# A two-layer hybrid encoder: 24 of the modulation sums of layer 0 move from VectorE to TensorE, beside the attention heads

## The chip, the cores and the metric

One Trainium2 chip, one of its cores. The metric is the device time of one execution in microseconds (us), the median of several executions. A core has TensorE (PE in the rows; its weight loads PEld), VectorE (DVE), ScalarE (ACT), GpSimd (POOL) and SyncE (SP); here SP only issues transfers. Each engine takes its instructions in the order in which the program was built.

## The reference

512 tokens of width 1024, two layers. Each layer takes six vectors from the conditioning `c`, 1024 wide each, that is 48 chunks of 128 numbers:

```python
c_act = jax.nn.silu(c)
mod = c_act @ w_mod[l] + b_mod[l]                 # 1024 -> 6144
sh1, sc1, g1, sh2, sc2, g2 = split(mod, 6)        # chunks 0-7, 8-15, 16-23, 24-31, 32-39, 40-47
h = rmsnorm(x, norm1[l]) * (1 + sc1) + sh1
u = h @ w_in[l]                                   # A: latent attention, B: dilated attention, C: S5
x = x + g1 * (concat(norm(o_a), norm(o_b), norm(o_c)) @ w_out[l])
h2 = rmsnorm(x, norm2[l]) * (1 + sc2) + sh2
x = x + g2 * conv_ffn(h2, ffn_w_up[l], ..., ffn_w_down[l])
```

So the first 16 chunks of layer 0 are wanted before the input projection, chunks 16 to 39 only after the attention: g1 when the output projection is added to x, sh2 and sc2 in the norm behind it.

## The kernel before

Activations lie transposed, 128 channels on the partitions and 512 tokens along a row. Every large product is three TensorE products of split operands (`mm3`, lines 378 to 380: high by high, low by high, high by low). A weight block comes by DMA into a `raw` tile (3 buffers), ScalarE casts its high part `wh` (line 372) and VectorE or GpSimd subtracts the low part `wl` (line 373); `wh` and `wl` have 4 buffers each.

A layer runs: input projection in three groups of output tiles (`u` in the rows; the first group has 6 output tiles and `w_in` blocks of 768 columns, the second 5 tiles and blocks of 640, the third 3 and 384), the S5 branch beside it (`bp`, `cp`, `bt`, `tm` are its tables, which go out to memory and come back; `oc` goes out and comes back as `U`; `s5s`, `s5y` are its products), six attention steps `n` of two heads each (dilated for n = 0 to 2, latent for n = 3 to 5), the output projection (`wo`), the norm and the feed-forward part. An attention step does, per 128 queries and head, scores (`sc`), the softmax pieces on VectorE and ScalarE (`P`, `nb`), four transposes (`pt`) and, per half, the product with the values (`pv`); `finish_pair` ends the step with a product on VectorE (line 1159, `ob` or `oa`). The work of the next heads is written beside each half (`side`).

The modulation sums are made in two ways:

- `mod_chunk` (line 328): a chunk of 128 columns comes in by a 512 KB transfer and one VectorE instruction multiplies it by the spread `c_act` and sums it. Chunks 16 to 39 of layer 0 are handed to `mixing` as `background`, two at a time: 12 are written in steps n = 3 to 5 (through `raw`), 12 beside the output projection (through `rawm`).
- `quad_rows` and `quad_cols` (lines 341 and 352): four chunks at once. Eight TensorE products `mq` take one column of `c_act`, 32 columns wide, against a 128x512 block of weights and add up in one bank; ScalarE copies the row out (`mrow`), four small products `mc` turn it into columns, two VectorE additions put in the bias. This is done for chunks 0 to 15, the 4 entries of `QUADS`: entry 0 ahead of the first group of the input projection, the others inside it by a rule on the block number `k`:

```python
q = k // 2 + 1
if q < len(QUADS) and k % 2 == 0 and i1 == nt:
    row, cur["pe"] = quad_rows(q, e)
elif q < len(QUADS) and k % 2 and i0 == 0:
    cur["pe"] = quad_cols(q, row, e)
```

The order on every engine is set when the program is built, by a scheduler that goes by priorities (`PRI`, `low(...)`) and by its own reckoning of when an instruction can start. On the chip each queue then runs in that order, and a transfer that waits for a buffer holds back all that are behind it on SP.

Of the kernel before, what the change touches and what calls it, by code (L numbers as in the profile page):

```python
# [11 lines left out]
F32R = mybir.dt.float32r  # L12
# [9 lines left out]
KD = D // 128  # L22
NH = 6
NPAIR = 22
PRI = {"xs": -400, "U1": 300, "ws": -200, "rs": -300, "cu": 10, "fin": 20, "glu": -30, "par": -30,
       "prep1": -20, "qk": 20, "rope": -20, "spread": -30}
MK = 2
OWN = 6
TOGETHER = 300
DQ = (0, 3, 0, 0)  # L30
QUADS = tuple((8 + 2 * q, 9 + 2 * q, 2 * q, 2 * q + 1) for q in range(4))
BLOCKS = ((0, 8), (8, 15), (15, 22))
EPS = 1e-6
MAGIC = 12582912.0
# [187 lines left out]
def program(ctx, tc, a, out):  # L222
    nc = tc.nc
# [34 lines left out]
    def as32(x):  # L258
        return x.bitcast(F32)
# [71 lines left out]
    def quad_rows(q, e):  # L331


        o = ps("mq")
        p_, nb = cur["modraw"]
        for t in range(4):
            r = p_.tile([128, 1024], F32, tag="rawm", name="rawm", bufs=nb)
            nc.sync.dma_start(r, a["wquad"][q, t])
            for k in (2 * t, 2 * t + 1):
                with after(e):  # L340
                    m = T.matmul(o[k % 4 * 32:k % 4 * 32 + 32], cth[:, k:k + 1].to_broadcast([128, 32]),
                                 r[:, k % 2 * 512:k % 2 * 512 + 512], start=k < 4, stop=k >= 4).ins
        row = p_.tile([128, 512], F32, tag="mrow", name="mrow", bufs=2)
        S.copy(row, o)
        return row, m

    def quad_cols(q, row, e):

# [449 lines left out]
    def mixing(l, background):  # L798
# [465 lines left out]
        def side(n):  # L1264

            if n == 0:
                for _ in range(2):
                    with low("dq"):
                        ahead.append(dil_qk(len(ahead)))
                    yield  # L1270
            elif n == 1:
                with low("qk"):
                    ahead.append(next_qk(0))
                with low("glu"):
                    s5_glu(l, mp, oc)
                yield
                with low("qk"):
                    ahead.append(next_qk(1))
            elif n == 2:
                with low("mc"):  # L1280
                    mix_group("mc", [oc[:, 0], oc[:, 1]], 6, (6, 7, 8, 9))
                yield
                with low("va"):
                    va.append(mla_values())
                with low("qk"):
                    ahead.append(next_qk(2))
            elif n == 3:
                with low("qk"):
                    ahead.append(next_qk(3))
                yield  # L1290
                with low("mb"):
                    mix_group("mb", ob, 3, range(6))
            elif n == 4:
                with low("qk"):
                    ahead.append(next_qk(4))
                yield
                with low("qk"):
                    ahead.append(next_qk(5))
            while True:
                yield  # L1300

        va = []
        for n in range(6):
            pr = n % 3
            sums = ap.tile([128, 8], F32, tag="sums", name="sums", bufs=2)
            o = ps("pv", "pv")
            beside = side(n)
            for half in range(2):
                PT = pt_tiles()
                for qt in (2 * half, 2 * half + 1):  # L1310
                    if n < 3:
                        S2 = scores2(*ahead[n], qt)
                    for hh in range(2):
                        if n < 3:
                            args = S2[hh], -0.125, K("bias", 384 - 128 * qt, 512)
                        else:
                            q, k, qs = ahead[3 + 2 * pr + hh]
                            args = scores(q, k, qt), qs[:, qt:qt + 1], None
                        unit(*args[:2], qt, hh, PT[hh], sums[:, hh * 4 + qt:hh * 4 + qt + 1], args[2])
                if n >= 3:  # L1320
                    background(2)
                with low("pv"):
                    pv(o[:, half * 256:half * 256 + 256], PT, dv if n < 3 else va[0], pr, half == 0, half == 1)
                catch_up()
                next(beside)
                catch_up()
            catch_up()
            if n >= 3:
                oa[pr] = ap.tile([128, N], F32, tag=f"ob{pr}", name=f"oa{pr}")
            with low("fin"):  # L1330
                finish_pair(o, sums, (oa if n >= 3 else ob)[pr])
# [217 lines left out]
    for l in range(L):  # L1549
        mod = lambda i, j0, j1: [lambda j=j: mod_chunk(i, j) for j in range(j0, j1)]  # L1550
        first = l == 0
        later = bg(mod(0, 16, 40) if first else [])
        mixing(l, later)
        later(100)
        nxt = bg((mod(0, 40, 48) if first else []) + (mod(l + 1, 0, 48) if l + 1 < L else []))
        ffn(l, nxt, prep(l + 1) if l + 1 < L else iter(()))
# [21 lines left out]
```

## Time and profile before

| | us |
|---|---|
| median of three timed runs | 1512.4 (1510.29 to 1515.06) |
| the profiled execution, its own time | 1503.78 |
| its span in the trace | 1502.0 |
| TensorE busy | 1394.0 (93%) |
| VectorE busy | 1040.3 (69%) |
| ScalarE busy | 693.0 (46%) |
| granted TensorE clock, mean | 0.961 of full speed |

The last 1.8 us of the profiled execution lie outside the span. Times of the trace are us from the span's start. A busy TensorE need not be at its peak, since the ends of pipelined products are modelled; the pitch from one start to the next tells how long one holds the engine.

### The profile page before, as it was taken

How to read it: one execution, taken by the hardware profiler on the slowest of the kernel's cores; microseconds unless marked ns; L12 is line 12 of the kernel's file. 1: busy time of each engine (PE TensorE's matmuls, PEld its weight loads, DVE VectorE, ACT ScalarE, POOL GpSimd, SP SyncE). 2: the span in 40 equal slices, each digit the busy share in tenths (PEclk: the TensorE clock that was granted, in tenths of full speed). 3: DMA queues.
4: the chain of work that ended last, by engine and by line, in shares of the span. 5: the costliest groups of instructions: out<-in, count | busy, mean ns of one | idle time of the engine just before them, and what ended most of it. 6: DMA issues, size and time to landing. Idle time of an engine off the chain costs nothing. (4 is left out here: it accounts for less than half of the span.)

```text
span 1502.0 us, 20427 instructions
## 1 busy us (share of the span) xinstructions
PE 1394.0 (93%) x7260; PEld 1120.1 (75%) x7260; DVE 1040.3 (69%) x2122; ACT 693.0 (46%) x1351; POOL 342.3 (23%) x290
## 2 busy tenths in 40 slices
PE   6889889888899999999999988898899999999998
PEld 3677656658878778887888766566698888888887
DVE  6687888856698779788647585667548663663663
ACT  4464365652454434444446335666445432442441
POOL 1274241310222153242134343223110000000000
PEclk9889999989999999999999999999999999999999
DMA  7746323105556477386336332000041333323322
GB/s 259 238 150 207 96 61 118 58 1 173 170 184 213 137 243 250 113 252 207 103 110 196 92 118 80 19 18 10 9 131 57 98 98 89 96 93 102 99 90 93
DMA packets 79398, 185.11 MB, mean 123 GB/s; under 512 B 12864, under 2 KB 38208, under 8 KB 79296
## 3 DMA queue, kind: packets, MB, share of 16 engines
q1 hardware_dynamic: 77856, 181.37, 38.2%
q10 hardware_dynamic: 1440, 2.44, 0.5%
q8 instruction: 57, 0.93, 0.3%
q14 instruction: 45, 0.37, 0.1%
HBM read 165.95 MB, written 15.73 MB: 121 GB/s over the span
## 5 line engine op out<-in xcount | busy, mean ns | idle before, releaser
L372 ACT CAST wh<-raw 128x512 fp32r<-128x512 f32 (+3 forms) x400 | 222.4, 567 | 303.3 <-PE dn L380 125.5
L373 DVE TENSOR_TENSOR wl<-raw,wh 128x512 fp32r<-128x512 f32 (+3 forms) x312 | 212.1, 683 | 121.7 <-ACT wh L372 121.1
L378 PE MATMUL up<-t,wh 128*128 128x512 f32 (+1 forms) x736 | 279.4, 381 | 2.5 <-ACT t L472 2.2
L379 PE MATMUL up<-t,wl 128*128 128x512 f32 (+1 forms) x736 | 279.3, 381 | 2.5 <-DVE wl L373 2.4
L380 PE MATMUL up<-t,wh 128*128 128x512 f32 (+1 forms) x736 | 278.2, 381 | 1.1 <-DVE t L473 1.0
L373 POOL TENSOR_TENSOR wl<-raw,wh 128x384 fp32r<-128x384 f32 (+1 forms) x88 | 112.1, 1277 | 228.1 <-ACT wh L372 216.5
L379 PEld LDWEIGHTS up<-t,wl 128*128 128x128 f32 x736 | 138.2, 188 | 30.8 <-DVE wl L373 3.6
L378 PEld LDWEIGHTS up<-t,wh 128*128 128x128 f32 x736 | 138.3, 188 | 30.1 <-ACT t L472 3.7
L380 PEld LDWEIGHTS up<-t,wh 128*128 128x128 f32 x736 | 137.2, 188 | 28.8 <-DVE t L473 2.4
L379 PE MATMUL dn<-gh,wl 128*128 128x512 f32 (+1 forms) x366 | 142.2, 390 | 1.6 <-DVE wl L373 1.6
L378 PE MATMUL dn<-gh,wh 128*128 128x512 f32 (+1 forms) x366 | 142.4, 391 | 0.0
L380 PE MATMUL dn<-gl,wh 128*128 128x512 f32 (+1 forms) x366 | 142.2, 390 | 0.0
L378 PE MATMUL u<-t,wh 128*128 128x512 f32 (+1 forms) x248 | 96.8, 400 | 7.5 <-ACT wh L372 5.1
L328 DVE CUSTOM_DVE_ANT_0 rawm<-rawm,cact,cols 128x1024 f32<-128x1024 f32 x68 | 91.2, 1344 | 14.9 <-DMA rawm<-in_wmod 14.5
L379 PE MATMUL u<-t,wl 128*128 128x512 f32 (+1 forms) x248 | 98.5, 398 | 2.0 <-POOL wl L373 1.3
L380 PE MATMUL u<-t,wh 128*128 128x512 f32 (+1 forms) x248 | 95.7, 391 | 2.6 <-DVE t L473 2.5
L1125 ACT ACTIVATE P<-P,nb 128x512 f32<-128x512 f32 x96 | 69.1, 721 | 35.3 <-DVE nb L1123 30.3
L379 PEld LDWEIGHTS dn<-gh,wl 128*128 128x128 f32 x366 | 68.7, 188 | 17.5 <-DVE wl L373 2.5
L378 PEld LDWEIGHTS dn<-gh,wh 128*128 128x128 f32 x366 | 68.7, 188 | 15.8 <-ACT gh L1468 0.7
L380 PEld LDWEIGHTS dn<-gl,wh 128*128 128x128 f32 x366 | 68.4, 188 | 15.6 <-DVE gl L1469 0.8
L1488 DVE SCALAR_TENSOR_TENSOR xs<-dn,modv,xs 128x512 f32<-128x512 f32 (+1 forms) x50 | 36.1, 726 | 44.1 <-PE dn L380 44.1
L1129 PE MATMUL pt<-cst,P 128*128 128x128 f32 x384 | 61.8, 289 | 3.4 <-ACT P L1125 2.9
(446 smaller groups left out, 2770.2 us busy)
## 6 DMA issues: line engine op xcount, KB each, us to landing
raw<-in_w_up SPq DMA_DIRECT2D x88, 512.0 KB, 3.8
rawm<-in_wmod SPq DMA_DIRECT2D x68, 512.0 KB, 4.4
raw<-in_w_dn SPq DMA_DIRECT2D x32, 448.0 KB, 3.3
rawm<-in_wquad SPq DMA_DIRECT2D x16, 512.0 KB, 6.2
raw<-in_w_dn SPq DMA_DIRECT2D x16, 512.0 KB, 3.7
raw<-in_w_in SPq DMA_DIRECT2D x40, 192.0 KB, 2.7
raw<-in_wmod SPq DMA_DIRECT2D x12, 512.0 KB, 3.7
raw<-in_w_in SPq DMA_DIRECT2D x16, 320.0 KB, 3.2
```

The source lines that it names most:

```text
L328: V.tensor_tensor_reduce(out=r, in0=r, in1=cact, scale=1.0, scalar=col(l, "bmod", j), op0=mul, op1=add, accum_out=modv[l][:, j:j + 1])
L372: S.copy(hi[:, :n], src)
L373: (eng or V).tensor_tensor(lo[:, :n], src, as32(hi[:, :n]), sub)
L378: T.matmul(o, wh, xh, start=first, stop=False)
L379: T.matmul(o, wl, xh, start=False, stop=False)
L380: return T.matmul(o, wh, xl, start=False, stop=last).ins
L1125: S.activation(P, P, AF.Exp, scale=-1.0, bias=nb, accum_out=sums)
L1129: T.transpose(t_ps[:, c], P[:, c], ident)
L1488: return V.scalar_tensor_tensor(xs[:, m, c], o, modv[l][:, 40 + m:41 + m], xs[:, m, c], mul, add).ins
```

## The change

`QUADS` gets six more entries, for chunks 16 to 39, and the weights in `in_wquad` grow with it. A new function `quad_late` loads an entry in eight transfers of 256 KB straight into four `wh` and four `wl` buffers; half an attention step later it does the eight `mq`, the copy and `quad_cols`, at a priority 20 below the rest. Step `n` of layer 0 issues the loads of entry `4 + n` after its first half and the products after its second. The 24 `mod_chunk` of layer 0 are gone from `background`.

```diff
-QUADS = tuple((8 + 2 * q, 9 + 2 * q, 2 * q, 2 * q + 1) for q in range(4))
+QUADS = tuple((8 + 2 * q, 9 + 2 * q, 2 * q, 2 * q + 1) for q in range(4)) + tuple(
+    tuple(range(j, j + 4)) for j in range(16, 40, 4))
...
+    def quad_late(q):
+
+        parts = []
+        for k in range(KD):
+            t = "wh" if k < 4 else "wl"
+            parts.append(strm.tile([128, 512], F32R, tag=t, name=t, bufs=4))
+            nc.sync.dma_start(as32(parts[k]), a["wquad"][q, k // 2, :, k % 2 * 512:k % 2 * 512 + 512])
+        yield
+        o = ps("mq")
+        for k in range(KD):
+            T.matmul(o[k % 4 * 32:k % 4 * 32 + 32], cth[:, k:k + 1].to_broadcast([128, 32]), as32(parts[k]),
+                     start=k < 4, stop=k >= 4)
+        row = tmp("rb", bufs=2)
+        S.copy(row, o)
+        quad_cols(q, row, None)
...
-            beside = side(n)
+            beside, quad = side(n), quad_late(4 + n)
...
+                if l == 0:
+                    with low("quad"):
+                        next(quad, None)
...
-        later = bg(mod(0, 16, 40) if first else [])
+        later = bg([])
```

The rule on `k` in the input projection reads `len(QUADS)`, which is now 10 and not 4. At k = 6 and k = 7 it asks for entry 4, which the rule did not do before: entry 4 (chunks 16 to 19) is now loaded and summed there too, and once more in attention step 0.

The order on SP before, from the first `w_in` block of the second projection group (128x640) to the first loads of `U` (`s5d` are the S5 tables that go out to memory, `cols` and `bc` constants):

```order
L310 DMA raw<-in_w_in 128x640
L668 DMA s5d_95<-bt 128x2x256 x2
L310 DMA raw<-in_w_in 128x640
L615 DMA bc<-in_s5b 128x4x64
L609 DMA s5d_95<-ei 128x2x256
L609 DMA s5d_95<-er 128x2x256
L609 DMA s5d_95<-ei 128x2x256
L609 DMA s5d_95<-er 128x2x256
L310 DMA raw<-in_w_in 128x640
L967 DMA U<-oc 32x2x128 x5
```

Three of the 640 blocks stand ahead of the first load of `U` here. The same place on SP after the change, from the last piece of S5 constants (`ht`) to the first 640 blocks:

```order
L515 DMA ht<-in_pos 128x512
L984 DMA U<-oc 32x2x128 x6
L685 DMA s5d_95<-bt 128x2x256 x2
L984 DMA U<-oc 32x2x128 x2
L689 DMA s5d_95<-tm 128x2x256
L984 DMA U<-oc 32x2x128 x8
L992 DMA cols<-in_cols 128x316
L311 DMA raw<-in_w_in 128x640 x2
```

No 640 block stands ahead of the sixteen loads of `U` any more. Further up on SP, the four loads of entry 4 (`rawm<-in_wquad`) now stand between the last two 768 blocks of the first group.

The order on TensorE before, at the seam between the first projection group (`u_277` to `u_282`) and the second (`u_961` to `u_965`):

```order
L380 MATMUL u_282<-t_274,wh 128x512
L647 MATMUL btp<-cst,bp_379 128x128 x8
L378 MATMUL u_961<-t_259,wh 128x512
L379 MATMUL u_961<-t_259,wl 128x512
L380 MATMUL u_961<-t_260,wh 128x512
L378 MATMUL u_962<-t_259,wh 128x512
L652 MATMUL tps<-cp_380,bp_379 128x128 x8
L906 MATMUL dsq<-cst,sqd 128x2 x4
L379 MATMUL u_962<-t_259,wl 128x512
```

The products of the second group stand between the S5 transposes (`btp`, `tps`) and the sums of squares (`dsq`). The same seam after the change (the second group is `u_987` to `u_991`):

```order
L397 MATMUL u_282<-t_274,wh 128x512
L664 MATMUL btp<-cst,bp_379 128x128 x8
L669 MATMUL tps<-cp_380,bp_379 128x128 x8
L923 MATMUL dsq<-cst,sqd 128x2 x16
L304 MATMUL cb<-cst,cth 128x128 x8
L429 MATMUL bc_959<-cst,bx 128x128 x4
L429 MATMUL bc_977<-cst,bx 128x128 x4
L395 MATMUL u_987<-t_259,wh 128x512
```

Before, 40 products of the second group stood ahead of the two `bc`, which spread the inverse roots of the dilated queries and keys; now none does.

On TensorE after the change, inside attention step 4, where entry 8 is summed and entry 9 begins:

```order
L397 MATMUL sc<-kl,qh 128x512
L358 MATMUL mq<-wh,cth 32x512 x4
L358 MATMUL mq<-wl,cth 32x512
L1146 MATMUL pt<-cst,P 128x128 x4
L358 MATMUL mq<-wl,cth 32x512 x3
L369 MATMUL mc<-cst,rb 128x1
L419 MATMUL bc<-cst,rks 128x128 x4
L369 MATMUL mc<-cst,rb 128x1 x3
L429 MATMUL bc_3362<-cst,bx 128x128 x4
L358 MATMUL mq<-wh,cth 32x512
```

The other five entries stand in the same way between scores, transposes and spreads: those of n = 0 and n = 1 ahead of the last `pv` of step 2, those of n = 2 to 5 behind it, the last one just ahead of the first products of the output projection.

## Rows read from the trace of the kernel before

**Rows 1.** First line of the page.

```profile
span 1502.0 us, 20427 instructions
```

**Rows 2.** Attention: ends of dilated and latent steps, layer 0 first, then layer 1.

```profile
L1159 DVE TENSOR_TENSOR ob<-pv,rb x3: 677/685/690, 216.2 to 279.8; 128x512 f32<-128x512 f32 x3
L1159 DVE TENSOR_TENSOR oa<-pv,rb x3: 683/683/692, 300.5 to 344.1; 128x512 f32<-128x512 f32 x3
...
L1159 DVE TENSOR_TENSOR ob<-pv,rb x3: 681/690/692, 959.1 to 1015.6; 128x512 f32<-128x512 f32 x3
L1159 DVE TENSOR_TENSOR oa<-pv,rb x3: 683/684/692, 1037.4 to 1078.2; 128x512 f32<-128x512 f32 x3
```

**Rows 3.** First and last addition of the output projection to x, both layers.

```profile
L1357 DVE SCALAR_TENSOR_TENSOR xs<-wo,modv,xs x16: 466/476/484, 389.0 to 405.7; 128x256 f32<-128x256 f32 x16
...
L1357 DVE SCALAR_TENSOR_TENSOR xs<-wo,modv,xs x16: 468/476/486, 1114.9 to 1130.8; 128x256 f32<-128x256 f32 x16
```

**Rows 4.** Stretches: busy us of PE, PEld, DVE, ACT, POOL, granted clock, DMA share, GB/s.

```profile
216.20:279.80 63.60, 58.26 (x336) 40.13 (x337) 53.85 (x147) 42.48 (x92) 11.39 (x9) 0.95 0.36 108
279.80:344.10 64.30, 54.41 (x313) 37.71 (x312) 39.75 (x105) 32.20 (x67) 16.46 (x13) 0.87 0.04 14
...
959.10:1015.60 56.50, 53.19 (x326) 37.66 (x325) 35.85 (x112) 38.85 (x82) 10.67 (x8) 0.97 0.04 12
1015.60:1078.20 62.60, 53.11 (x323) 37.90 (x322) 40.28 (x108) 34.48 (x73) 16.52 (x13) 0.92 0.02 6
```

**Rows 5.** Stretches of the output projection, the same columns.

```profile
344.10:389.00 44.90, 37.08 (x271) 35.99 (x271) 29.63 (x67) 10.68 (x23) 2.85 (x3) 0.89 0.61 200
...
385.00:389.00 4.00, 4.00 (x21) 4.00 (x21) 0.59 (x2) 1.50 (x3) 0.00 (x0) 0.54 0.49 153
1078.20:1114.90 36.70, 34.19 (x277) 33.77 (x277) 14.96 (x36) 11.18 (x23) 0.00 (x0) 0.95 0.25 71
```

**Rows 6.** TensorE's timeline at 382.70, with idle before and releaser.

```profile
382.70 0.80 PE L378 MATMUL wo<-qh,wh 128*128 128x256 f32 x2 [4.96 <-ACT wh L372]
```

**Rows 7.** Who waited for whom, ScalarE, 344 to 389: total, times, longest.

```profile
ACT wh L372 <- DMA raw<-in_w_out: 14.5, 2, 8.6
```

**Rows 8.** VectorE's groups, 150 to 420: busy, mean ns, idle before.

```profile
L328 DVE CUSTOM_DVE_ANT_0 raw<-raw,cact,cols 128x1024 f32<-128x1024 f32 x12 | 17.4, 1452 | 1.3 <-DMA raw<-in_wmod 1.3
```

**Rows 9.** TensorE's timeline, 62 to 67.2: the last entry of QUADS.

```profile
62.20 1.92 PE L341 MATMUL mq<-rawm,cth 128*32 128x512 f32 x16
...
66.25 0.95 PE L352 MATMUL mc<-cst,mrow 128*128 128x1 f32 x8
67.05 0.48 PE L378 MATMUL u<-t,wh 128*128 128x512 f32 x1
```

**Rows 10.** SP's timeline, 60 to 100: start, length, transfer.

```profile
67.66 0.40 SPq L310 DMA_DIRECT2D raw<-in_w_in  x1
...
82.16 3.30 SPq L967 DMA_DIRECT2D U<-oc  x5
...
89.40 6.22 SPq L967 DMA_DIRECT2D U<-oc  x8
```

**Rows 11.** Transfers by line: number, KB each, us from issue to landing.

```profile
raw<-in_w_in SPq DMA_DIRECT2D x16, 320.0 KB, 3.2
```

**Rows 12.** Products of the projection (tile u) alone: TensorE busy, clock.

```profile
82.50:102.10 19.60, 10.00 (x27) 0.74 0.39 113
```

**Rows 13.** TensorE's timeline, 118 to 119: two products of the second group.

```profile
118.15 0.39 PE L378 MATMUL u<-t,wh 128*128 128x512 f32 x1
118.38 0.39 PE L379 MATMUL u<-t,wl 128*128 128x512 f32 x1
```

**Rows 14.** Stretches behind the seam, columns as in rows 4.

```profile
90.00:100.00 10.00, 8.15 (x35) 6.97 (x34) 9.77 (x18) 6.00 (x12) 6.20 (x6) 0.59 0.31 83
130.00:180.00 50.00, 42.10 (x238) 35.48 (x237) 47.14 (x102) 19.32 (x43) 19.37 (x16) 0.93 0.41 128
```

**Rows 15.** VectorE's timeline: its first work on the S5 products.

```profile
125.77 0.69 DVE L743 TENSOR_TENSOR m<-s5s,s5wer 128x512 f32<-128x512 f32 x1 [0.88 <-DMA s5wer<-s5d]
```

More of the change, by code (lines that the diff above doesn't have):

```diff
@@ L25 @@
 PRI = {"xs": -400, "U1": 300, "ws": -200, "rs": -300, "cu": 10, "fin": 20, "glu": -30, "par": -30,
-       "prep1": -20, "qk": 20, "rope": -20, "spread": -30}
+       "prep1": -20, "qk": 20, "rope": -20, "spread": -30, "quad": 20}
 MK = 2
```

## The prediction

> **What bounds the kernel now.** I read the totals first: the span is 1502.0 us [rows 1] and the profiled execution took 1503.78, 8.6 under the median of the runs, 1512.4. TensorE is busy 93% of it, by the table. The change touches layer 0 up to the output projection alone, and layer 1 runs the same six attention steps and the same output projection without these 24 sums beside them. So I used layer 1 as a measure of what layer 0 would be without them, and read three places.
>
> First, attention. The last instructions of the steps [rows 2] cut it into stretches. From the end of step 0 to the end of step 2, layer 0 takes 63.6 us and layer 1 takes 56.5 [rows 4]. TensorE is busy 58.26 and 53.19 of them, VectorE 53.85 and 35.85. The difference on VectorE, 18.0, is the 12 sums that ran there (17.4, 1452 ns each) [rows 8]. From the end of step 2 to the end of step 5, layer 0 takes 64.3 and layer 1 62.6, with TensorE busy 54.41 and 53.11 [rows 4]. TensorE is the bound of the dilated steps, with 5.3 and 3.3 us idle; in the latent steps it is idle for 9.9 of 64.3.
>
> Second, the output projection. From the end of the last step to the first addition to x [rows 2, 3], layer 0 takes 44.9 us and layer 1 36.7 [rows 5]. The reader is to see where the 8.2 go: at 382.70 TensorE has stood idle for 4.96 us for the high part of a weight block [rows 6], ScalarE had waited 14.5 us in two waits for the transfers of `w_out` [rows 7], which stand on SP among the loads of the sums; and in 385 to 389 the granted clock is 0.54 [rows 5], which is mostly the lower of its levels, 1.2 GHz.
>
> Third, the seam between the first two groups of the input projection, which the diff does not mention but the order shows.
>
> **The change part by part.**
>
> *The output projection.* The last 12 sums and their 12 transfers of 512 KB leave it. VectorE loses 12 instructions of 1.45 us there (29.63 busy in layer 0, 14.96 in layer 1 [rows 5]), and the `w_out` blocks find an empty queue. The stall is worth at least its 4.96 us; with the clock as in layer 1 the stretch becomes 36.7. I take −8.2, with −5.0 as the other end. What could eat it: entry 9 is loaded through `wh` and `wl`, so the first splits of `w_out` wait until its products have read them. These stand just ahead of the projection's products on TensorE, so I put that wait with the next part.
>
> *Attention.* Removed: 12 sums on VectorE. By layer 1 the dilated stretch would lose 7.1 us. That holds only if VectorE's work was what stretched it; TensorE's own busy time, 58.26 to 53.19, says that 5.1 of the 7.1 were slower or stretched products, so the figure is an upper end of the gain, and I keep it since the number of products is nearly the same (336 and 326). Added: six quads. The last quad of the input projection shows the price on TensorE: its eight `mq` (two passes each, 16 records) take 1.92, and the `mc` 0.80, from 66.25 to the next product at 67.05 [rows 9]. A quad is 2.7 us, six are 16.2. The 48 transfers of 256 KB carry what 24 of 512 KB did; the copies on ScalarE and the twelve small VectorE additions lie beside other work, ScalarE being busy 42.48 of 63.6 and 32.20 of 64.3 [rows 4].
>
> How much of 16.2 hides in TensorE's idle time? At most 3.3 in the dilated stretch and 9.9 in the latent ones, 13.2, so that 3.0 stay: −7.1 + 3.0 = −4.1. At least nothing: −7.1 + 16.2 = +9.1. The order shows the quads as runs of three to five products between scores, transposes and spreads, so an `mq` whose weights are late holds the head's products too; an idle gap is filled only where it happens to stand. I take 1 us hidden of the two quads in the dilated stretch and 5, half of the idle time, of the four behind it: 16.2 − 6 − 7.1 = **+3.1**.
>
> *The fifth quad.* Entry 4 is now summed in the input projection as well: 2.7 us of TensorE [rows 9] in a stretch where products follow each other, and 2 MB ahead of the last 768 block. This is the lower end of what the start costs: +2.7.
>
> *The reordered start.* Before, SP issued the first 640 block at 67.66, ahead of the `U` loads that run from 82.16; the last eight start at 89.40 and keep SP 6.22 more, to 95.62 [rows 10]. All sixteen wait on a chain (products, `oc` out, back), so whatever stands behind them waits too. Now the first 640 block stands behind all of them. I let the `U` loads come 1.5 later than before, about half of the fifth quad: SP is free at 97.1; the block takes 3.2 us to land [rows 11], 100.3; the cast and the subtraction, 0.7 each as a VectorE instruction of 128x512 [rows 15], bring the first product of the second group to about 102. In the trace of before 27 products of that group stood done by 102.1, which had filled TensorE's gaps [rows 12]. They are now to be done behind it: 27 by the 0.23 us pitch of [rows 13] is 6.2. The clock is not full there: in 90 to 100, with TensorE waiting on and off, it was 0.59 [rows 14]. Eight products at half clock add 8 by 0.23, or 1.8. Together **+8.0**. With all 27 at half clock it would be 12.4, less the 1.5 of delay if the `U` loads come as before: +10.9 is the upper end. Other work of the seam does not fill the gap, since the S5 transposes, the sums of squares and the spreads stand in the gap in both programs.
>
> The Trainium skill, "TensorE: Matmul & The Clock Gate", section "HAM oscillation — how this bites in real kernels", speaks against this change at the seam: a TensorE that stands and waits for loads between groups of products drops to its lower clock, and pays for the wait a second time. By that rule the sum stays as above; without it the 1.8 would fall away and the time be 1513.5. The trace agrees with the rule, with 0.54 behind the stall of 4.96 us [rows 5, 6].
>
> Does the lag last? VectorE begins on the S5 products at 125.77 [rows 15] and is busy 47.14 of the 50 us from 130 to 180, TensorE 42.10 [rows 14]. So VectorE can win back at most 2.9 before attention. I carry the whole lag, since idle time that is spread over 50 us is seldom of use; 2.9 less is inside the range.
>
> *Sum:* 8.0 + 3.1 − 8.2 = +2.9 us. 1503.78 + 2.9 = 1506.7 for an execution like the profiled one, and with the 8.6 between it and the median, **1515**.
>
> **The rivals.**
>
> *A, the forecast:* three terms that nearly cancel, 1515.3.
>
> *B, the quads are exposed.* TensorE runs in order, and each quad waits on transfers that are issued behind buffers which the attention's own splits free. Nothing hides: +8.0 + 9.1 − 8.2 = +8.9, 1521.3. It is slower by more than 0.3% (4.5 us, about what these runs can tell from no change) as soon as less than 4.4 of the 16.2 is hidden. For it: the dilated steps have TensorE busy over 90%. Against: 9.9 idle in the latent steps.
>
> *C, the quads fit the gaps.* +8.0 − 4.1 − 8.2 = −4.3, 1508.1; with a lag of 7.8 or less it is faster by over 0.3%, and with VectorE winning back 2.9 it is 1505.2. For it: VectorE, freed of 17.4 us [rows 8], may have been what made TensorE wait in layer 0, and layer 1's TensorE has 12.8 us idle between the same steps [rows 4]. Against: the gaps are many, and a quad is written as runs of three to five products, not as one piece for one gap.
>
> *D, a fuller TensorE keeps its clock.* In layer 0's latent steps the granted clock was 0.87, in layer 1's 0.92, and those took 1.7 us less [rows 4]; with quads filling the gaps, layer 0 may come to that: 2.9 − 1.7 = +1.2, 1513.6. The Trainium skill, same page, section "Part 1: The HAM clock gate (the "warmup" mystery)", has the rule behind this: sustained work brings the array's clock back to the full 2.4 GHz. The rows here bear out only the falling side.
>
> *That the change does not do what it says:* for entry 4 it does it twice; that is in the sum.
>
> **How the numbers follow.** A 0.36, B 0.32, C 0.26, D 0.06. The likeliest gives 1515; its own range, with 3 us to either side for the lag and the hidden share, is 1512 to 1518. The range must reach to B and C: 1505 to 1523 leaves out the lower part of C (lag near 2.7) and the upper of B (lag near 10.9), about 0.2. Faster: most of C (0.20) and 0.02 of A with a small lag, 0.22. Slower: B but for 0.01, and 0.03 of A with a large lag, 0.34. The same: what is left, 0.44.
>
> **What would show it.** The start: the first product of the second projection group near 102, with TensorE idle ahead of it behind SP's `U` loads, and VectorE's first S5 work 8 us after 125.77; if that comes within 3 us, the lag is wrong. Attention: six groups of `mq` and `mc`, with the end of step 0 to the end of step 2 near 61 us, and step 2 to step 5 near 70; near 57 and 64 it is C, over 62 and 75 it is B. The output projection: no stall of 5 us on `wh`, and 36.7 from the last step to the first addition; if ScalarE still waits there for `w_out`, now for buffers that entry 9 holds, the −8.2 is wrong. Wrong altogether would be a lag that VectorE wins back whole, or a wait on the quads' loads of several us in each step, which neither layer of before can show.

## The result, and the profile of the changed kernel

The changed kernel takes 1528.8 us (median of 4 runs, 1525.1 to 1533.6) beside 1511.4 of the kernel before on the same chip: a ratio of 1.0143, 95% interval 1.0114 to 1.0171, or 17 us slower. The forecast was 1515 with a range to 1523; the slowdown is outside it. The profiled execution took 1530.14 us. Its span is longer than that of [rows 1] by 26.4; the difference between that and 17 is that the profiled execution of before was one of its shorter ones (1503.78 beside a median of 1511.4) and that of the changed kernel lay 1.4 above its median.

Page of the changed kernel, first lines:

```profile
span 1528.4 us, 20819 instructions
## 1 busy us (share of the span) xinstructions
PE 1421.3 (93%) x7428; PEld 1136.3 (74%) x7428; DVE 1013.7 (66%) x2088; ACT 697.5 (46%) x1358; POOL 335.1 (22%) x290
```

VectorE's 1040.3 busy us became 1013.7, TensorE's 1394.0 became 1421.3: the sums moved as intended. The time went in three places of layer 0 (the seam, attention, and the norm behind the output projection), and each has rows that answer to those of before.

The seam at the start. SP's timeline in the changed kernel, then TensorE's, then VectorE's, and last the first attention scores (start, length, instruction, idle before and who ended it):

```profile
88.79 5.88 SPq L984 DMA_DIRECT2D U<-oc  x8
...
95.39 0.86 SPq L311 DMA_DIRECT2D raw<-in_w_in  x2
```

```profile
100.96 1.97 PE L429 MATMUL bc<-cst,bx 128*128 128x128 f32 x8 [4.79 <-ACT bx L425]
102.58 0.78 PE L395 MATMUL u<-t,wh 128*128 128x512 f32 x1
...
112.22 0.66 PE L664 MATMUL btp<-cst,bp 128*128 128x128 f32 x4 [1.53 <-DVE glv L950]
112.64 0.48 PE L395 MATMUL u<-t,wh 128*128 128x512 f32 x1
117.48 3.70 PE L669 MATMUL tps<-cp,bp 128*128 128x128 f32 x16 [4.36 <-ACT bt L665]
```

```profile
139.62 0.69 DVE L760 TENSOR_TENSOR m<-s5s,s5wer 128x512 f32<-128x512 f32 x1 [1.08 <-PE s5s L747]
```

```profile
199.47 0.50 PE L1193 MATMUL sc<-kh,qh 64*128 64x512 f32 x2
```

The first 640 block is issued behind the last load of `U`, and the first product of the second group comes at 102.58; the prediction said near 102. Thirty products of the group are done by 110.3. But TensorE stands again behind them, 1.53 and 4.36 us: the next S5 transposes (`btp`, `tps`) wait for VectorE and ScalarE. The `tps` at 117.48 wait for ScalarE's copy of `bt`, which stands there behind its copies of the fourth and last `cp` table. These rows in the changed kernel, and then the copy of that table in before:

```profile
113.35 0.41 ACT L652 COPY cp<-u 64x256 f32<-64x256 f32 x1 [0.53 <-DVE u L648]
...
116.85 1.06 ACT L665 COPY bt<-btp 128x512 f32<-128x512 f32 x2
```

```profile
105.94 0.82 ACT L635 COPY cp<-u 64x256 f32<-64x256 f32 x2
```

The fourth table is copied 7.4 us later than in before. (The third is copied earlier, at 84.97 and not 96.53, so it is not what the transposes lack.) So VectorE's first S5 work is 13.9 late, not 8 ([rows 15] has 125.77), and so are the first scores. Their row in before:

```profile
185.29 0.50 PE L1176 MATMUL sc<-kh,qh 64*128 64x512 f32 x2
```

The lag is 14.2 there. (A second profile of before has its first scores at 182.47, so a single start is good to some 3 us.) The stretches from then on, in the changed kernel: first scores to the end of step 0, to the end of step 2, to the end of step 5, to the first addition to x, to the last piece of the norm behind it (columns as in [rows 4]):

```profile
199.50:238.40 38.90, 34.70 (x184) 20.66 (x183) 30.93 (x67) 24.91 (x55) 15.69 (x11) 0.81 0.22 65
238.40:297.10 58.70, 56.55 (x361) 40.21 (x360) 35.98 (x111) 37.16 (x77) 12.02 (x9) 0.95 0.26 82
297.10:369.20 72.10, 64.71 (x392) 39.69 (x391) 41.39 (x127) 36.63 (x78) 15.26 (x13) 0.93 0.25 84
369.20:406.60 37.40, 34.78 (x282) 34.37 (x282) 15.09 (x38) 11.30 (x24) 2.84 (x3) 0.95 0.28 81
406.60:439.50 32.90, 29.35 (x212) 28.18 (x211) 22.45 (x59) 17.26 (x41) 10.25 (x12) 0.90 0.34 108
```

Before, the first and the last of these were, by the same rows of its trace:

```profile
185.30:216.20 30.90, 25.77 (x142) 15.47 (x141) 27.55 (x59) 20.25 (x44) 15.42 (x11) 0.89 0.13 37
...
L470 DVE SCALAR_TENSOR_TENSOR ht<-xs,g_n,bc x16: 461/472/479, 403.2 to 418.7; 128x256 f32<-128x256 f32 x16
```

The reader is to see: 8.0 more to the end of step 0 (38.9 for 30.9), 4.9 less in the dilated stretch and 7.8 more in the latent one [rows 4], 7.5 less in the output projection [rows 5], and 3.2 more behind it (32.9, where before took 418.7 − 389.0 = 29.7). With 14.2 at the start this is +20.8 by the end of the norm. The last 5.6 of the 26.4 arise in layer 1, where no instruction was changed; the last section has them. The 3.2 behind the output projection go with the clock: it was 1.00 there in before and 0.90 here, and run 7 below, with the same late quads and a clock of 1.00 there, took 30.1.

### The profile page after: what moved, and what is told of

It is laid out like the page before. It is cut to its first block, busy times and chain, and to the rows that moved or that the text cites. A ratio compares the mean times of both kernels' runs of the same rounds, so it can differ in the third digit from the quotient of the medians.

```text
span 1528.4 us, 20819 instructions
## 1 busy us (share of the span) xinstructions
PE 1421.3 (93%) x7428; PEld 1136.3 (74%) x7428; DVE 1013.7 (66%) x2088; ACT 697.5 (46%) x1358; POOL 335.1 (22%) x290
## 5 line engine op out<-in xcount | busy, mean ns | idle before, releaser
L395 PEld LDWEIGHTS up<-t,wh 128*128 128x128 f32 x736 | 138.3, 188 | 29.7 <-ACT t L489 3.7
L1142 ACT ACTIVATE P<-P,nb 128x512 f32<-128x512 f32 x96 | 69.1, 721 | 36.7 <-DVE nb L1140 29.7
L329 DVE CUSTOM_DVE_ANT_0 rawm<-rawm,cact,cols 128x1024 f32<-128x1024 f32 x56 | 75.4, 1348 | 9.8 <-DMA rawm<-in_wmod 9.6
L396 PEld LDWEIGHTS dn<-gh,wl 128*128 128x128 f32 x366 | 68.8, 188 | 17.4 <-DVE wl L390 2.4
L395 PEld LDWEIGHTS u<-t,wh 128*128 128x128 f32 x248 | 49.4, 201 | 22.4 <-ACT wh L389 8.6
```

The lines of the kernel that those rows point to most:

```text
L329: V.tensor_tensor_reduce(out=r, in0=r, in1=cact, scale=1.0, scalar=col(l, "bmod", j), op0=mul, op1=add, accum_out=modv[l][:, j:j + 1])
L395: T.matmul(o, wh, xh, start=first, stop=False)
L396: T.matmul(o, wl, xh, start=False, stop=False)
L1142: S.activation(P, P, AF.Exp, scale=-1.0, bias=nb, accum_out=sums)
```

## The experiments

All ratios are to the kernel before on the same chip, with 95% intervals; 0.001 is 1.5 us.

**1. The rule back at 4.**

```diff
-                        if q < len(QUADS) and k % 2 == 0 and i1 == nt:
+                        if q < 4 and k % 2 == 0 and i1 == nt:
...
-                        elif q < len(QUADS) and k % 2 and i0 == 0:
+                        elif q < 4 and k % 2 and i0 == 0:
```

> The changed kernel with q < 4 in place of q < len(QUADS) in the input projection: no fifth quad there, and the start is in the order of before on every engine. Theory 1 (the start lost 14.2 us by the first attention scores, 185.3 to 199.5, and all of it reaches the end): the time falls by about 14 from 1528.8, to 1512 to 1517, and the first scores come within 1 us of 185.3. Rival (most of the lag of the start is made up later, since VectorE has no sums left in attention, and the six late quads are what costs): less than 5 us come back, 1524 or more, although the first scores are back at 185.

Measured: 1.0037 (1.0014 to 1.0060), 1511.5 us; the first scores at 183.25, 2.0 sooner than expected and inside what executions of one kernel differ by. Of the 1.43%, 1.06 are gone with the fifth quad, so the lag of the start is not made up later, and the rival falls. The ends of the steps and the first addition in it:

```profile
L1176 DVE TENSOR_TENSOR ob<-pv,rb x3: 676/680/687, 222.7 to 283.7; 128x512 f32<-128x512 f32 x3
L1176 DVE TENSOR_TENSOR oa<-pv,rb x3: 690/690/692, 307.7 to 357.3; 128x512 f32<-128x512 f32 x3
L1377 DVE SCALAR_TENSOR_TENSOR xs<-wo,modv,xs x16: 473/476/484, 392.5 to 412.2; 128x256 f32<-128x256 f32 x16
```

Attention, from the first scores to the end of step 5, takes 174.0 us, and 158.8 in before (185.29 to 344.1).

**2. The ten entries alone,** in the kernel before.

```diff
-QUADS = tuple((8 + 2 * q, 9 + 2 * q, 2 * q, 2 * q + 1) for q in range(4))
+QUADS = tuple((8 + 2 * q, 9 + 2 * q, 2 * q, 2 * q + 1) for q in range(4)) + tuple(
+    tuple(range(j, j + 4)) for j in range(16, 40, 4))
```

> The kernel before with the ten entries of QUADS and nothing else of the change: the rule loads and sums the fifth quad in the input projection (chunks 16 to 19, summed again later as before), the start is in the order of the changed kernel, and the 24 sums stay on VectorE. Theory 1: slower than before by 11 to 15 us, 1522 to 1526, first scores near 199. Rival (the lag is made up later): at most 5 us slower. If only the work of the fifth quad counted and not the new order, it would be 2.7 us slower.

Measured: 1.0094 (1.0061 to 1.0128), 14 us slower, the first scores at 201.57. Runs 1 and 2 add up: 0.37% and 0.94% are 1.31, beside 1.43 for both. The fifth quad, which the diff does not name, is two thirds of the cost.

**3. No late quads, and no sums at all in their place,** on run 1.

```diff
-                if l == 0:
-                    with low("quad"):
-                        next(quad, None)
```

> The changed kernel with the rule at 4 and without the six late quads: chunks 16 to 39 of layer 0 are not summed at all (zeros stand in their place). The price of the six quads is the difference to the run with the rule at 4. Theory 1 (the quads stand exposed on TensorE, 12 of their 16.2 us: 2.2 in the dilated stretch and 9.5 in the latent one over layer 1): 10 to 14 us below that run, about 1501. Rival (the quads fit the idle time and attention is late for the start's sake): at most 5 below it. Both expect the output projection stretch near 37 us, as in layer 1.

Measured: 0.9915 (0.9890 to 0.9939), 12.8 us faster than before. The late quads cost 1.0037 − 0.9915, or 18.4 us, good to some 5 us: about their 16.2 on TensorE or a little more. The same kernel was run once more for its trace.

> The run without quads once more, for its trace (no sums of chunks 16 to 39): by theory 1 the stretch from the end of step 0 to the end of step 2 is 56 to 58 us and that from step 2 to step 5 is 62 to 64, as in layer 1, and the output projection to the first addition 35 to 37. Rival (the sums on VectorE did not stretch attention): 62 or more for the dilated stretch.

The stretches in it, from the first scores at 185.28 to the end of step 0, of step 2, of step 5, and to the first addition:

```profile
185.30:216.00 30.70, 25.82 (x142) 15.37 (x141) 27.57 (x59) 20.25 (x44) 15.43 (x11) 0.89 0.10 29
216.00:279.40 63.40, 57.86 (x331) 41.37 (x332) 39.65 (x120) 41.14 (x89) 10.46 (x9) 0.92 0.07 22
279.40:343.10 63.70, 54.05 (x318) 38.23 (x318) 39.17 (x109) 33.52 (x70) 16.44 (x13) 0.89 0.02 6
343.10:375.70 32.60, 32.47 (x278) 32.22 (x278) 14.99 (x38) 11.23 (x24) 2.85 (x3) 1.00 0.31 90
```

Here the rival is right about attention. Without any sum the dilated stretch takes 63.4 us, where before took 63.6 with 12 of them [rows 4]: VectorE's 17.4 us cost nothing there that can be seen, and the 7.1 that layer 1 suggested were not to be had. (The granted clock was 0.92 here and 0.95 in before, so a us or two of gain could be hidden in this one stretch; over all of attention it was 0.90 in both, with 157.8 and 158.8 us.) What there is to win lies in the output projection: 32.6 for 44.9, and of that 9.8 by the end of the norm (343.1 to 407.9, for 344.1 to 418.7).

**4. All 24 sums on VectorE in attention,** in the kernel before.

```diff
                 if n >= 3:
-                    background(2)
+                    background(4)
```

> The kernel before with all 24 sums written in attention steps 3 to 5, four at a time and not two, and none beside the output projection: the part of the change that frees the output projection, without TensorE doing any of it. If the output projection is held up by the loads of its 12 sums, that stretch falls from 44.9 to about 37, and VectorE, busy 39.75 of 64.3 in the latent stretch, has room for 17.4 more there: 5 to 8 us faster than before, 1503 to 1506. Rival: the sums in attention hold up VectorE's softmax work, and the stretch from the end of step 0 to the end of step 5 grows by 8 us or more, so that nothing is won.

Measured: 1.0031 (1.0010 to 1.0052), slower. The gain of the theory and the loss of the rival both come, and nothing is won: the output projection falls to 35.3 (351.0 to 386.3), and attention, from the first scores to the end of step 5, grows from 158.8 to 168.4:

```profile
L1159 DVE TENSOR_TENSOR ob<-pv,rb x3: 674/685/691, 213.3 to 282.9; 128x512 f32<-128x512 f32 x3
L1159 DVE TENSOR_TENSOR oa<-pv,rb x3: 685/690/691, 310.6 to 351.0; 128x512 f32<-128x512 f32 x3
L1357 DVE SCALAR_TENSOR_TENSOR xs<-wo,modv,xs x16: 469/476/484, 386.3 to 405.7; 128x256 f32<-128x256 f32 x16
...
182.64 0.51 PE L1176 MATMUL sc<-kh,qh 64*128 64x512 f32 x2
```

The first 12 sums cost attention 1.0 us (158.8 beside 157.8 without any), the second 12 cost 9.6.

**5. The quads' products without their loads,** and **6. the loads without the products,** both on run 1.

```diff
-            parts.append(strm.tile([128, 512], F32R, tag=t, name=t, bufs=4))
-            nc.sync.dma_start(as32(parts[k]), a["wquad"][q, k // 2, :, k % 2 * 512:k % 2 * 512 + 512])
+            parts.append(cact[:, k % 2 * 512:k % 2 * 512 + 512])
...
-            T.matmul(o[k % 4 * 32:k % 4 * 32 + 32], cth[:, k:k + 1].to_broadcast([128, 32]), as32(parts[k]),
+            T.matmul(o[k % 4 * 32:k % 4 * 32 + 32], cth[:, k:k + 1].to_broadcast([128, 32]), parts[k],
```

> The run with the rule at 4, but the six late quads are computed from a tile that is resident (the spread c_act) and not from loaded weights: no loads of entries 4 to 9 and no use of the wh and wl tiles, so chunks 16 to 39 come out as other sums. All products, copies and additions of the quads stay. Theory 1 (the 18.4 us that the six quads cost between the run with the rule at 4 and the run without quads are TensorE's time, 16.2 us of it by the trace): 14 to 18 us above the run without quads, a ratio to before of 1.000 to 1.004. Rival (the loads through the split tiles make the attention's own splits wait, and the products wait on the loads): at most 6 us above the run without quads, a ratio of 0.995 or less.

Measured: 0.9969 (0.9944 to 0.9995): 8.1 us above the run without quads.

```diff
-        o = ps("mq")
-        for k in range(KD):
-            T.matmul(o[k % 4 * 32:k % 4 * 32 + 32], cth[:, k:k + 1].to_broadcast([128, 32]), as32(parts[k]),
-                     start=k < 4, stop=k >= 4)
-        row = tmp("rb", bufs=2)
-        S.copy(row, o)
-        quad_cols(q, row, None)
+        for k in range(KD):
+            V.tensor_copy(modv[0][:, 16:17], as32(parts[k])[:, :1])
```

> The run with the rule at 4, with the loads of entries 4 to 9 through the wh and wl tiles and half a step later one copy of a single column on VectorE from each of these tiles, but no products, no row copy and no additions: chunks 16 to 39 are not summed (zeros). Theory 1: as the run without quads within 3 us, a ratio of 0.990 to 0.994. Rival (loads and tiles cost): 10 us or more above it, a ratio of 0.998 or more.

Measured: 0.9953 (0.9928 to 0.9978), 5.7 above it. Neither theory holds alone: by these times the products without loads cost half of their 16.2, and the loads without products cost something of their own. Each of these differences is good to some 5 us, so that the 4.6 by which both together (18.4) exceed the sum of the two (13.8) are not clear of noise. One would think that each holds up the other. SP's waits in run 1, 180 to 365, suggest it:

```profile
SPq L354 <- PE mq L358: 72.0, 6, 24.8
SPq L311 <- DVE sml L1097: 27.8, 3, 18.9
SPq L311 <- DVE wl L390: 22.2, 4, 17.7
SPq L354 <- PE gg L397: 20.4, 1, 20.4
```

A quad's loads stand on SP until the quad before has left the tiles (72.0 us in six waits), and everything behind them on SP stands too. But TensorE does not feel it: in attention (first scores to the end of step 5) its list of waits in run 1 has none for a quad's load and none for a split `wh` or `wl`; the largest are 4.1 us in four waits for `nb` and 3.2 for a copied `pt`, both of VectorE. Attention takes 174.0 us in run 1 and 164.8 in run 5, with the same products (935 and 933 records). Of the 9.2 between them TensorE is idle for 2.5; for 6.8 it is longer busy. The sums over attention and the dilated stretch of each, run 1 first:

```profile
222.70:283.70 61.00, 59.64 (x361) 42.21 (x360) 36.02 (x111) 37.24 (x76) 12.04 (x9) 0.89 0.24 80
sum 174.10, PE 158.76 PEld 103.78 DVE 109.16 ACT 99.10 POOL 42.98; mean PE 39.69 PEld 25.95 DVE 27.29 ACT 24.78 POOL 10.75
```

```profile
222.70:279.70 57.00, 54.98 (x367) 39.15 (x365) 38.36 (x117) 39.72 (x83) 12.04 (x9) 1.00 0.05 18
sum 164.80, PE 151.95 PEld 99.22 DVE 108.52 ACT 98.56 POOL 42.96; mean PE 37.99 PEld 24.80 DVE 27.13 ACT 24.64 POOL 10.74
```

The granted clock over all of attention was 0.89 in run 1 and 0.93 in run 5; the changed kernel, with the same quads and loads as run 1, had 0.91 and took 169.7, with TensorE busy for 156.0. So the same products take longer where the clock is slower, and whether the loads make the clock slower or the execution does is not shown.

**7. The quads' loads on GpSimd's queue,** on run 1.

```diff
-            nc.sync.dma_start(as32(parts[k]), a["wquad"][q, k // 2, :, k % 2 * 512:k % 2 * 512 + 512])
+            nc.gpsimd.dma_start(as32(parts[k]), a["wquad"][q, k // 2, :, k % 2 * 512:k % 2 * 512 + 512])
```

> The run with the rule at 4, with the 48 loads of the six late quads issued by GpSimd and not by SyncE. Of the 18.4 us that the quads cost, products on resident data account for 8.1 and loads with a small reader for 5.7 by the two runs before this; SyncE stood in a quad load for 72 us in six waits on earlier quad products. Theory 1 (a quad load that waits for its tile holds back the attention's own blocks on SyncE): 4 to 9 us come back, a ratio to before of 0.998 to 1.001. Rival (the tiles themselves are short: four high and four low parts taken by a quad leave none for the attention's splits, and GpSimd's own subtractions now wait behind the loads): within 2 us of the run with the rule at 4, 1.002 to 1.006, or slower.

Measured: 1.0033 (1.0011 to 1.0056), as run 1. The 4 to 9 us do not come back, and theory 1 fails, with a reserve: GpSimd itself now stands 17.9 us in three waits for the tiles. That the tiles are short, the rival, is only argued: a version with eight tiles of its own was not run, and TensorE's waits in run 1 do not speak for it.

**8 to 10. Why the start costs 14 us.** Three ways of having the fifth quad, all on run 2: its loads without its products, its products without its loads, and all of it at a priority 400 lower.

```diff
-                        if q < len(QUADS) and k % 2 == 0 and i1 == nt:
+                        if q == 4 and k % 2 == 0 and i1 == nt:
+                            p_, nb = cur["modraw"]
+                            for t in range(4):
+                                x5 = p_.tile([128, 1024], F32, tag="rawm", name="rawm", bufs=nb)
+                                nc.sync.dma_start(x5, a["wquad"][q, t])
+                        elif q < 4 and k % 2 == 0 and i1 == nt:
```

```diff
-            r = p_.tile([128, 1024], F32, tag="rawm", name="rawm", bufs=nb)
-            nc.sync.dma_start(r, a["wquad"][q, t])
+            if q < 4:
+                r = p_.tile([128, 1024], F32, tag="rawm", name="rawm", bufs=nb)
+                nc.sync.dma_start(r, a["wquad"][q, t])
+            else:
+                r = xs[:, t * 2:t * 2 + 2].rearrange("p a b -> p (a b)")
```

```diff
-                            row, cur["pe"] = quad_rows(q, e)
+                            with low("q5" if q > 3 else "none"):
+                                row, cur["pe"] = quad_rows(q, e)
```

> The run with the ten entries and nothing else of the change, with the loads of the fifth quad kept and its products, copy and additions left out: TensorE does none of it (the sums of chunks 16 to 19 come later, as before, so nothing is missing). The order at the seam is almost that of the run with the ten entries: no 640 block ahead of the U loads, the two spreads bc ahead of the second group. Theory 1 (the order of the seam costs, not the 2.7 us of the quad on TensorE): 10 to 15 us slower than before, a ratio of 1.007 to 1.010. Rival (the fifth quad's products inside the first group cost, by what they hold up): within 4 us of before.

> The run with the ten entries and nothing else of the change, with the products of the fifth quad taken from the resident x and not from loaded weights (its two additions write sums that are overwritten later by the right ones): 2.7 us of TensorE in the first group, no loads. The order has two 640 blocks ahead of the U loads, as before has three. Theory 1: 2 to 5 us slower than before, a ratio of 1.001 to 1.004. Rival (the fifth quad's work on TensorE is the cause, whatever the order): 10 us or more slower, 1.007 or more.

> The run with the ten entries and nothing else of the change, but the fifth quad is built at a low priority (400 below the rest): it is loaded and summed all the same, its loads and products stand later in the queues, and two of the 640 blocks stand ahead of the U loads again. Theory 1 (the 14 us of the start come from the order at the seam, not from the fifth quad's own 2.7 us): 2 to 6 us above before, a ratio of 1.001 to 1.004. Rival (the fifth quad's work and its 2 MB of loads at a time when transfers are short): 10 to 14 us above before, as in the run with the ten entries alone.

Measured: 1.0085 (1.0053 to 1.0117), 1.0101 (1.0066 to 1.0136), 1.0141 (1.0105 to 1.0176). With none of the quad's work on TensorE the loss is 13 us, so its 2.7 us are not the cause. But the products alone cost as much, against theory 1: two 640 blocks ahead of the `U` loads did not save that start. The third separates nothing, since it has a stall of its own, where TensorE waits 11.80 us for loads that were issued late:

```profile
84.51 4.46 PE L342 MATMUL mq<-rawm,cth 128*32 128x512 f32 x12 [11.80 <-DMA rawm<-in_wquad]
```

The seam is best measured from its first `btp` to the first scores, since executions of one kernel come to that `btp` at different times (82.17 and 76.61 in two profiles of before). The `btp` in before and in run 8, and the first scores of run 8:

```profile
82.17 1.03 PE L647 MATMUL btp<-cst,bp 128*128 128x128 f32 x8
```

```profile
76.87 1.04 PE L648 MATMUL btp<-cst,bp 128*128 128x128 f32 x8
...
191.15 0.76 PE L1182 MATMUL sc<-kh,qh 64*128 64x512 f32 x2
```

That is 103.1 us in before (105.9 in its second profile) and 114.3 in run 8, 113.1 in run 9, 118.2 in run 2 and 117.5 in the changed kernel. So 8 to 11 us of the loss are there without the quad's products (run 8), and 7 to 10 without its loads (run 9). Neither is needed for it; a new order of the seam is what both have. They do not lose it at one place: run 8 waits 5.4 us ahead of the spreads `bc`, as the changed kernel does (4.79), run 9 waits 0.2 there but 3.9 for an S5 table that comes back from memory. That the order costs, and not the quad's work on TensorE, is what these runs favour; which of the moved instructions it is, they do not show.

The first of the three had a riddle of its own: by its first scores (191.15) and the end of its norm (422.4 beside 418.7) it was only 4 to 6 us late, and lost the rest in layer 1. So it and the kernel before were profiled again.

> The kernel with the fifth quad's loads alone, profiled a second time. In the first profile the norm behind layer 0's output projection ended 3.7 us later than in before and the stretch in layer 1 took 175.6 us, 12 more than in before. Theory 1 (the seam costs some 6 to 14 us, by its order, and layer 1 varies by execution): the norm ends 4 to 15 us later than in before, and the stretch in layer 1 is 164 to 171. Rival (the late loss belongs to this kernel): the stretch in layer 1 is 174 or more again.

> The kernel before, profiled a second time. If the long stretch of layer 1's norm and projection in other runs (from the end of layer 0's feed-forward part to the end of layer 1's attention step 0: 163.7 us in the first profile of before, 164 to 176 in the others) is a matter of the execution, this one differs from 163.7 by some us with the same instructions; if it belongs to the kernel, it is within 1 us of 163.7. The first attention scores of layer 0 come within 3 us of 185.3 in either case.

Measured: the first scores at 193.26 and 182.47, the norm's end at 427.8 and 415.2. From the first `btp` to the first scores the kernel takes 114.7 (114.3 the first time) and before 105.9 (103.1), so that the seam costs 8 to 12 us, and the first profile looked better because it came to the seam early. The stretch in layer 1 is 174.6 for that kernel (175.6 the first time), and 166.9 for before (163.7). The rival is right: 7.7 us or more of the late loss come again with the kernel, and 3.2 is what two executions of before differ by; see the last section.

**11. The loads of the 12 sums beside the output projection on GpSimd's queue,** in the kernel before.

```diff
-            nc.sync.dma_start(r, a["wmod"][l, j])
+            (nc.gpsimd if l == 0 and 16 <= j < 40 else nc.sync).dma_start(r, a["wmod"][l, j])
```

> The kernel before, with the transfers of the 24 sums that go through rawm or raw tiles in layer 0 unchanged but for one thing: the 12 beside the output projection are issued by GpSimd and not by SyncE, so that a load that waits for its tile holds back no w_out block. Theory 1 (the 4.96 us stall of the output projection in before is the queue: w_out blocks stand behind loads of sums): the stall goes, the stretch from the last step to the first addition falls from 44.9 to 37 to 40, and the kernel is 4 to 7 us faster, a ratio of 0.995 to 0.997. Rival (the stretch is bound by what the loads move, 200 GB/s there, or by VectorE's 17.4 us of sums): the stall only changes its place, and the time is within 2 us of before.

Measured: 0.9964 (0.9934 to 0.9995), 5.4 us faster than before and just clear of no change, with all sums still on VectorE. The stall is gone, and TensorE has no wait of 1 us or more in the last 23 us of the stretch; but that takes 41.5 us and not 37 to 40, so the queue alone gives back 3.4 of the 8.2:

```profile
341.60:383.10 41.50, 37.60 (x297) 36.39 (x296) 29.69 (x67) 10.87 (x23) 7.86 (x12) 0.96 0.55 178
```

This is the one version with all sums right that beats both kernels.

**12. The same with 18 sums in attention and 6 beside the output projection.**

```diff
                 if n >= 3:
-                    background(2)
+                    background(3)
```

> The kernel before with the loads of the sums beside the output projection issued by GpSimd, and 18 of the 24 sums written in attention steps 3 to 5 (three at a time) and 6 beside the output projection. If the sums in attention are nearly free until VectorE's idle time is used up (12 cost 1 us, 24 cost 10 by the trace), 18 cost 2 to 5 and the output projection gives 3 to 5 more than with 12 beside it: a ratio to before of 0.993 to 0.997, at or below the run with the GpSimd queue alone (0.9964). Rival (each sum beyond 12 costs the 0.8 us that the 24 showed): 0.997 to 1.000.

Measured: 1.0009 (0.9985 to 1.0032): the rival, or a little worse. Attention takes 166.3 (183.40 to 349.7), 7.5 more than before, and the output projection gives 10.7 back (34.2 for 44.9) but 2.3 are lost behind it (32.0 for 29.7); the sums in attention are nearly free up to 12 and no further.

## Why the prediction was wrong

The sum was 8.0 + 3.1 − 8.2 = +2.9, and the measured value is +17. The order of the work was read rightly, the fifth quad among it; two terms failed, each in one step, and one loss was not priced.

- **The start, +8.0; measured 14** (14.2 at the first scores, 0.94% in run 2). What the term priced came as forecast: the first product at 102.58 for "about 102", and thirty products by 110.3. The failed step is that the sum ends there: "Other work of the seam does not fill the gap, since the S5 transposes, the sums of squares and the spreads stand in the gap in both programs". Two more sets of the transposes stand behind it, and the wait for them was put at nothing. They cost TensorE 1.53 and 4.36 us of waiting, and sixteen `tps` took 3.70 us where they take 2.05 in before, at a granted clock of 0.55 from 117.4 to 121.4. That the lag reaches the end was right.
- **Attention, +3.1; measured +10.9**, and +15.2 in run 1 (174.0 for 158.8). The failed step: "By layer 1 the dilated stretch would lose 7.1 us". Without any sum it loses 0.2, and all of attention 1.0. The prediction called 7.1 an upper end and kept it "since the number of products is nearly the same (336 and 326)". But the two stretches do not hold the same work: ScalarE does 22 of the softmax pieces `P` in layer 0's and 19 in layer 1's. In proportion, an estimate, 19 pieces would take 54.9 of the 63.6 us, and layer 1 took 56.5. The other half, "16.2 − 6", came out near: from run 3's trace to the changed kernel attention grows by 11.9 (157.8 to 169.7), where 10.2 were forecast, and TensorE's idle time there falls by 6.4 (20.1 to 13.7). In run 1 attention grows by 16.2, with 4.7 of idle time filled and the products slower.
- **The output projection, −8.2; measured −7.5** to the first addition. It was right as to place, and as to cause in part: run 11 takes away the queue alone, the stall goes, and 3.4 of the stretch with it; the rest goes only with the sums themselves (32.6 in run 3, 35.3 in run 4). Behind it 3.2 were lost, which the prediction did not price, and the same is seen without quads (32.2, 375.7 to 407.9). The clock behind it was 0.90 in the changed kernel, 0.95 in run 3 and 1.00 in before.
- **The rivals.** B had the right side. Its +9.1 for attention lies near the measured +10.9, but by two errors against each other: it too counted on the 7.1, and it hid nothing where 6.4 us of idle time were filled. It lacked the 6 of the start and the 3.2. C needs quads that cost 3 us and is excluded by run 3. D's clock of 0.92 in the latent stretch did come (0.93) and saved nothing that could be seen.

## What to carry to other kernels

Search a change for the names it lengthens: a rule on `len(QUADS)` that nobody touched cost two thirds of the loss, and only the order showed it. A twin stretch elsewhere (layer 1 for layer 0) says what a stretch may take, not why it takes longer here; count that both hold the same work, and leave the work out once before you count on winning it. Where a queue makes TensorE wait, move the transfers to another queue before you move the computation: that won 5.4 us in run 11, and nothing in run 7, where TensorE had no such wait. Before you look for a wait, see whether the engine was idle longer or busy longer with the same products.

## What the runs showed of the hardware

The granted clock can fall with TensorE busy all the time by the profile. In layer 1's projection, some 40 us behind the end of layer 0's feed-forward part, the kernel with the fifth quad's loads has 4 us at full clock with TensorE busy all of them, and 4 us later the lower level, 1.2 GHz; and so over 20 us a mean of 0.74:

```profile
837.30:841.30 4.00, 4.00 (x19) 3.31 (x18) 0.54 (x3) 1.85 (x4) 1.06 (x2) 1.00 0.50 131
845.30:849.30 4.00, 4.00 (x16) 3.52 (x15) 0.51 (x2) 0.51 (x1) 0.77 (x1) 0.50 0.29 82
841.30:861.30 20.00, 20.00 (x95) 17.00 (x94) 6.45 (x21) 6.37 (x13) 5.72 (x6) 0.74 0.19 52
```

The same 20 us in the kernel before, and in the changed one:

```profile
835.40:855.40 20.00, 18.33 (x106) 15.15 (x106) 10.91 (x27) 7.47 (x16) 8.60 (x7) 1.00 0.23 68
```

```profile
854.50:874.50 20.00, 20.00 (x103) 17.06 (x102) 7.80 (x25) 6.57 (x13) 6.18 (x6) 0.83 0.29 77
```

The instructions are the same in all three, in the same order on TensorE, VectorE, ScalarE and GpSimd. Both profiles of the first have 0.74, both of before 1.00; runs 9, 11 and 12 have 0.74 too, runs 4, 7 and 10 have the changed kernel's 0.83, runs 1, 2, 3, 5 and 6 have 1.00. From the end of layer 0's feed-forward part to the end of layer 1's step 0 the kernels at 1.00 take 163.7 to 168.7 us, those at 0.83 take 168.9 to 171.1, those at 0.74 take 169.9 to 175.6. So a change in layer 0 can cost some us in layer 1 that go with the clock. The changed kernel takes 169.3 there, 5.6 more than the 163.7 of before. Part of that is of this kind, as far as these rows go, but run 1 takes 168.7 at 1.00, so not all of it need be. What starts such a spell was not found.
